# A decoder layer on one core: the start of VectorE's work reordered, a second tile taken without norms, and a last product over four held chunks

## The chip, the cores and the metric

One Trainium2 chip, one of its cores. The metric is the device time of one execution in microseconds (us). The kernel before took 766.85 us (median of 3 runs, 766.26 to 767.05). One more execution was profiled: it took 766.03 us, of which the trace covers 764.2 us from the first to the last instruction.

A core has five engines that run side by side, each through its own queue in order: TensorE (PE, matmuls; PEld is its weight load), VectorE (DVE), ScalarE (ACT), GpSimd (POOL) and SyncE (SP, which here issues the transfers). They wait for each other through semaphores.

## The reference

The layer norms `x` (512 rows of 1024), multiplies it with one wide matrix, mixes tokens in three branches, adds the result to `x`, and then runs a gated MLP. Cut to what matters here:

```python
h = rms_norm(x, g_mix)
proj = h @ w_in
q, k, v, qi, ki, wi, conv_in, qc, gate_pre = split_cols(proj, PROJ_SIZES)
qi, ki = partial_rope(qi, ...), partial_rope(ki, ...)      # the indexer: it picks 128 keys per query
y_att = dsa_attention(q, k, v, qi, ki, wi) @ w_att_out
bg, cg, u = jnp.split(conv_in, 3, axis=-1)                 # 384 channels each: three tiles of 128
y_conv = (bg * causal_dwconv(cg * u, conv_w_short)) @ w_conv_out
y_mem = memory_attention(qc, km, vm) @ w_mem_out
x = x + merged @ w_o
up = causal_dwconv(rms_norm(x, g_ffn) @ w_up, conv_w_ffn)
x = x + (silu(gate) * val) @ w_down
return rms_norm(x, g_final)
```

The norm of a row of `x` is one number per row, so `(x*g) @ w` times that number is the same as `h @ w`.

## The kernel before, in words

Activations lie turned, channels on the 128 partitions and the 512 rows along the free axis. Every operand of a large product is split into a high and a low part (`hi` on ACT by a copy, L160 and L361 and L368; `lo` on DVE by a subtraction, L161, L362, L369), and a product is three matmuls: high by high, low by high, high by low (L150 to L152). A projection of one tile of 128 output channels (`project`, L460) is thus 8 chunks of 3 = 24 matmuls of 512 columns into one PSUM bank. The banks come in three pools: `mm` with 3, `at` with 4, `o` with 1. In the first part one `mm` bank (and `o`) holds the memory's keys and values until ACT reads them at L515 and L516, so two `mm` banks are left for the projections, and a projection waits until the bank it takes has been read.

The order of work. Up to L450 most instructions are in the order in which they are written (`keep`); after that a scheduler sets the order. What is written:

- The rows' norms come out as `rb` (one number per row, on all partitions) and `rx`. The values `v` and the indexer's operands are a product `pn` of unnormed `x` (`xh`, `xl`) that is multiplied by `rx` later.
- `h_split` (L356) makes one of eight chunks of `h`: DVE multiplies (L360), ACT copies the high part (L361), DVE subtracts (L362), each step waiting for the one before.
- The first tile of `cg` (`C_CG`) is taken from unnormed `x` (L409 to L413), and `cg0` is that times `rb` (L430). All other tiles are `project(...)` of `h`: `C_U`, `C_BG`, then the second tiles `C_CG + P`, `C_U + P` and so on (L578 to L596).
- The indexer's rows `rn` are scaled, get the rotary step (L422 to L427), are turned by PE (L433 to L439), and are laid out as `K4` and `Q4`: 16 copies of 32 partitions on ACT (L504) and 19 small transfers on SP. PE then scores them (L525).
- After its product the second tile of `cg` is read from its bank by ACT (`rr`, L585).

At the end `stream_rows` (L814) multiplies `act` with `w_down`: 22 chunks of weights stream through three buffers; for the first 19 chunks PE goes over all 8 output banks per chunk, the last 3 chunks are held, and PE finishes one bank after the other. `after_down` (L903) then adds the bank to `x`, squares and sums on ACT (L910), takes the power on POOL (L918), and writes the normed rows (L919, L920).

Of the kernel before, what the change touches and what calls it, by code (L numbers as in the profile page):

```python
# [93 lines left out]
def layer(ctx, tc, x, mem, g_ffn, g_final, w_in, x_n, m_kv, w_cm, w_att, w_o, w_up, w_down,  # L94
# [314 lines left out]
    pc = bank()  # L409
    for k in range(KD):  # L410
        wh, wl = (x[:, k, :] for x in ready[C_CG])
        for i, (a, b) in enumerate(((wh, xh[k]), (wh, xl[k]), (wl, xh[k]))):
            keep(nc.tensor.matmul(pc, a, b, start=k == 0 and i == 0, stop=k == KD - 1 and i == 2))  # L413
# [19 lines left out]
    for t in range(3):  # L433
        pt = bank("at")
        for b in range(NB):
            if t == 2:
# [3 lines left out]
        if t == 2:  # L440
            keep(nc.scalar.activation(rK, pt[:IDXD], AF.Copy))
        else:
            keep(nc.scalar.activation(rQ[:, t, :], pt[:, :SQ], AF.Copy))
    for b in range(NB):
        v = pn[b][:, :KV].rearrange("p (g d) -> p g d", g=NG)
        nc.scalar.activation(V[:, b, :, 0:HD], v, AF.Copy, scale=rx[:, b:b + 1])
        nc.vector.scalar_tensor_tensor(V[:, b, :, HD:], v, rx[:, b:b + 1], V[:, b, :, 0:HD].bitcast(F32), op0=ALU.mult,
                                       op1=ALU.subtract)
        nc.vector.tensor_scalar(wiN[:, b, :], pn[b][:, NW - NIH:NW], rx[:, b:b + 1], (NIH * IDXD) ** -0.5, op0=ALU.mult,
                                op1=ALU.mult)  # L450
# [527 lines left out]
```

## Time and profile before

| what | value |
|---|---|
| median of 3 runs | 766.85 us |
| profiled execution: own time, span of its trace | 766.03 us, 764.2 us |
| PE busy | 745.3 us (98%), 3443 matmuls |
| DVE busy | 473.2 us (62%) |
| ACT busy | 346.9 us (45%) |
| mean granted TensorE clock | 0.991 of full speed |

PE is busy for nearly the whole span, so the time can only shrink where PE is idle, runs at its lower clock, or has already ended. The profile shows three such places: a stretch between 42 and 78 us, the first microseconds, and the last 8 us behind the last matmul. The views used below are the busy time by stretch, the waits by engine, and the timeline. In a timeline a number behind the start is the duration; engines overlap the end of one instruction with the start of the next, so what an instruction costs in a row of its kind is the distance between two starts. `[2.19 <-ACT rr L585]` is idle time before the row, and who ended it.

### The profile page before, as it was taken

The page shows a single profiled execution, that of the slowest core. Times are in us where ns is not written, and L with a number is a line of the kernel's source. Part 1 is how long each engine was busy: PE and PEld are TensorE (multiplying, and loading weights), DVE is VectorE, ACT ScalarE, POOL GpSimd, SP SyncE. Part 2 cuts the span into 40 slices and gives each one's busy share as a digit, 9 for nine tenths or more (in the row PEclk, how much of TensorE's full clock was granted, in tenths as well). Part 3 has the DMA queues.
Part 4 walks back from the last instruction along what each step waited for, and adds up shares of the span by engine and source line. Part 5 has one row for each costly group of instructions (what it writes and reads, how often), then busy time and mean ns, then how long its engine had stood idle before and what let it go on. Part 6 is the DMA issues. An engine that isn't in the chain of part 4 may idle for free.

```text
span 764.2 us, 9125 instructions
## 1 busy us (share of the span) xinstructions
PE 745.3 (98%) x3443; PEld 620.8 (81%) x3443; DVE 473.2 (62%) x798; ACT 346.9 (45%) x576; POOL 18.0 (2%) x42
## 2 busy tenths in 40 slices
PE   9977999999999999999999999999999999999995
PEld 7955888888888888888889888888888888888884
DVE  5675899999677765367365656565656664222225
ACT  7649465657455653234335343434343433121214
POOL 0000002000000000000010000000000000000001
PEclk9998999999999999999999999999999999999998
DMA  9725233532221223443502223332222232323212
GB/s 344 283 78 163 78 104 117 156 107 72 73 83 65 71 74 107 155 133 108 193 28 84 90 104 90 103 93 100 97 97 98 95 101 70 124 92 100 93 29 110
DMA packets 25965, 83.38 MB, mean 109 GB/s; under 512 B 3297, under 2 KB 4449, under 8 KB 25921
## 3 DMA queue, kind: packets, MB, share of 16 engines
q1 hardware_dynamic: 25776, 82.53, 32.6%
q8 instruction: 27, 0.44, 0.2%
q10 hardware_dynamic: 144, 0.26, 0.1%
q14 instruction: 18, 0.14, 0.1%
HBM read 77.34 MB, written 2.10 MB: 104 GB/s over the span
## 4 chain that ended last, share of the span: by engine, by line
PE 88%; ACT 3%; DVE 2%; issue 1%; POOL 0%; POOLq 0%; ACTq 0%
PE ps_mm L150 18%; PE ps_mm L151 18%; PE ps_mm L152 18%; PE ps_at L150 9%; PE ps_at L152 9%; PE ps_at L151 9%; ACT Q L504 1%; PE ps_at L733 1%; PE ps_o L764 1%; PE ps_at L750 1%; PE ps_o L152 1%; PE ps_o L151 1%; PE ps_o L150 1%; PE ps_at L664 0%; PE ps_o L702 0%
## 5 line engine op out<-in xcount | busy, mean ns | idle before, releaser
L161 DVE TENSOR_TENSOR wlo<-raw,whi 128x1024 fp32r<-128x1024 f32 (+2 forms) x122 | 144.9, 1188 | 193.1 <-ACT whi L160 193.0
L160 ACT ACTIVATE whi<-raw 128x1024 fp32r<-128x1024 f32 (+2 forms) x122 | 125.7, 1031 | 184.6 <-PE ps_o L152 81.9
L150 PE MATMUL ps_mm<-hhi,whi 128*128 128x512 f32 x304 | 120.8, 397 | 3.8 <-ACT rr L585 2.2
L152 PE MATMUL ps_mm<-hhi,wlo 128*128 128x512 f32 x304 | 120.3, 396 | 0.3 <-DVE wlo L369 0.3
L151 PE MATMUL ps_mm<-hlo,whi 128*128 128x512 f32 x304 | 120.3, 396 | 0.2 <-DVE hlo L362 0.2
L151 PE MATMUL ps_at<-h2l,whi 128*128 128x512 f32 (+1 forms) x216 | 78.9, 366 | 0.0
L152 PE MATMUL ps_at<-h2h,wlo 128*128 128x512 f32 (+1 forms) x216 | 78.8, 365 | 0.0
L150 PE MATMUL ps_at<-h2h,whi 128*128 128x512 f32 (+1 forms) x216 | 78.7, 366 | 0.0
L150 PEld LDWEIGHTS ps_mm<-hhi,whi 128*128 128x128 f32 x304 | 57.8, 190 | 16.3 <-ACT rr L585 2.4
L152 PEld LDWEIGHTS ps_mm<-hhi,wlo 128*128 128x128 f32 x304 | 57.8, 190 | 12.4 <-DVE wlo L369 0.7
L151 PEld LDWEIGHTS ps_mm<-hlo,whi 128*128 128x128 f32 x304 | 57.8, 190 | 12.1 <-DVE hlo L362 0.5
L150 PE MATMUL ps_mm<-h2h,whi 128*128 128x512 f32 x160 | 62.2, 389 | 0.0
L151 PE MATMUL ps_mm<-h2l,whi 128*128 128x512 f32 x160 | 62.2, 389 | 0.0
L152 PE MATMUL ps_mm<-h2h,wlo 128*128 128x512 f32 x160 | 62.2, 389 | 0.0
L151 PEld LDWEIGHTS ps_at<-h2l,whi 128*128 128x128 f32 x216 | 40.8, 189 | 6.6
L152 PEld LDWEIGHTS ps_at<-h2h,wlo 128*128 128x128 f32 x216 | 40.8, 189 | 6.5
L150 PEld LDWEIGHTS ps_at<-h2h,whi 128*128 128x128 f32 x216 | 40.6, 189 | 6.5
L151 PEld LDWEIGHTS ps_mm<-h2l,whi 128*128 128x128 f32 x160 | 30.0, 188 | 6.3
L150 PEld LDWEIGHTS ps_mm<-h2h,whi 128*128 128x128 f32 x160 | 30.0, 188 | 6.2
L152 PEld LDWEIGHTS ps_mm<-h2h,wlo 128*128 128x128 f32 x160 | 30.0, 188 | 6.2
L897 ACT ACTIVATE t<-t 128x512 f32<-128x512 f32 x22 | 13.9, 633 | 44.5 <-DVE t L576 44.4
L160 ACT ACTIVATE acth<-t 128x512 fp32r<-128x512 f32 x14 | 8.8, 632 | 40.5 <-DVE t L898 40.5
(288 smaller groups left out, 1325.6 us busy)
## 6 DMA issues: line engine op xcount, KB each, us to landing
raw<-w_up SPq DMA_DIRECT2D x44, 512.0 KB, 3.5
raw<-w_in SPq DMA_DIRECT2D x39, 512.0 KB, 3.3
raw<-w_down SPq DMA_DIRECT2D x22, 512.0 KB, 3.5
raw<-w_o SPq DMA_DIRECT2D x8, 512.0 KB, 3.6
xn<-x_n SPq DMA_DIRECT2D x3, 937.0 KB, 12.2
raw<-w_cm SPq DMA_DIRECT2D x8, 320.0 KB, 3.0
rows<-x SPq DMA_DIRECT2D x4, 512.0 KB, 12.1
x<-x SPq DMA_DIRECT2D x4, 512.0 KB, 5.4
```

Of the source, the lines that this page charges most:

```text
L150: nc.tensor.matmul(o, sh, mh, start=first, stop=False)
L151: nc.tensor.matmul(o, sh, ml, start=False, stop=False)
L152: nc.tensor.matmul(o, sl, mh, start=False, stop=last)
L160: nc.scalar.activation(hi, src, AF.Copy)
L161: nc.vector.tensor_sub(lo, src, hi.bitcast(F32))
L504: nc.scalar.activation(Q4[32 * i:32 * i + 32, 4 * t + j, :], r[src], AF.Copy)
L733: nc.tensor.matmul(pb[:, :N], QS[:, hd, b * P:(b + 1) * P], KS[i][:, g, :N], start=(i == 0), stop=(i == 1))
L750: nc.tensor.transpose(pt[:, kb * P:(kb + 1) * P], lt[:, kb * P:(kb + 1) * P], ident)
L764: nc.tensor.matmul(po[:, q0:], V[:, kb, g, :], PT[i][:, c], start=(kb == 0 and i == 0), stop=(kb == NB - 1 and i == 1))
L897: nc.scalar.activation(tt[0], tt[0], AF.Silu)
```

## The change

`h` is built in a pipeline: `h_split` is taken apart into `h_rows` (multiply, copy) and `h_low` (subtract), and a piece's subtraction is written behind a later piece's multiplication. `ahead` (split of a weight tile) is likewise taken apart into `split_hi` (ACT) and `split_lo` (DVE). The first tile of `C_U` is now also taken from unnormed `x` (`bare`), as that of `C_CG` was; `cg0` becomes both products times `rb` twice, one DVE multiplication more. The rotary step, the turning and the layout of the indexer's operands stand earlier or in another order, and two second tiles of weights (`C_CG + P`, `C_U + P`) are loaded in the written part. In the last product 4 chunks are held instead of 3, in buffers of their own (those of `h2`), and the last bank is finished in two halves of 256 columns, the second half in a bank of its own.

```diff
     early(C_BG)
+    early(C_CG + P)
+    early(C_U + P)
...
-    def h_split(*ks):
-
-        for k in ks:
-            xt = xn[k // 2][:, k % 2, :S]
-            keep(nc.vector.scalar_tensor_tensor(xt, xt, xn[k // 2][:, k % 2, S + NW:], rb, op0=ALU.mult, op1=ALU.mult))
-            keep(nc.scalar.activation(h[0][:, k], xt, AF.Copy))
-            keep(nc.vector.tensor_sub(h[1][:, k], xt, h[0][:, k].bitcast(F32)))
+    def h_rows(k):
+
+        xt = xn[k // 2][:, k % 2, :S]
+        keep(nc.vector.scalar_tensor_tensor(xt, xt, xn[k // 2][:, k % 2, S + NW:], rb, op0=ALU.mult, op1=ALU.mult))
+        keep(nc.scalar.activation(h[0][:, k], xt, AF.Copy))
+
+    def h_low(k):
+        xt = xn[k // 2][:, k % 2, :S]
+        keep(nc.vector.tensor_sub(h[1][:, k], xt, h[0][:, k].bitcast(F32)))
...
-    h_split(0)
+    h_rows(0)
+    split_hi(C_CG)
     cols_split(3, [0, 1])
     rows_products(6, 7)
-    h_split(1)
-    ahead(C_CG)
-    h_split(2, 3, 4)
+    h_rows(1)
+    h_low(0)
+    split_lo(C_CG)
+    h_rows(2)
+    h_low(1)
+    h_rows(3)
+    h_low(2)
+    split_hi(C_U)
+
+    def bare(c0, ks):
+        pb = bare_banks.setdefault(c0, None) or bank()
+        bare_banks[c0] = pb
+        for k in ks:
+            wh, wl = (x[:, k, :] for x in ready[c0])
+            for i, (a, b) in enumerate(((wh, xh[k]), (wh, xl[k]), (wl, xh[k]))):
+                keep(nc.tensor.matmul(pb, a, b, start=k == 0 and i == 0, stop=k == KD - 1 and i == 2))
+        return pb
...
-    ahead(C_U)
-    h_split(5)
+    vs = [pn[b][:, :KV].rearrange("p (g d) -> p g d", g=NG) for b in range(NB)]
+    for b in range(NB):
+        keep(nc.scalar.activation(V[:, b, :, 0:HD], vs[b], AF.Copy, scale=rx[:, b:b + 1]))
+    split_lo(C_U)
...
+    h_rows(4)
     keep(nc.vector.tensor_mul(cg0, pc, rb))
-    h_split(6, 7)
-    ahead(C_BG)
+    h_low(3)
+    split_hi(C_BG)
+    h_low(4)
+    bare(C_U, range(5))
...
+    pu0 = bare(C_U, range(5, KD))
...
+    split_lo(C_BG)
+    h_rows(5)
+    h_rows(6)
+    h_low(5)
+    h_rows(7)
+    h_low(6)
+    keep(nc.vector.tensor_mul(cg0, pu0, cg0))
+    h_low(7)
+    split_hi(C_CG + P)
+    split_lo(C_CG + P)
+    keep(nc.vector.tensor_mul(cg0, cg0, rb))
...
+    qls = [halves(rQ[:, t, :], ip, SQ)[1] for t in range(2)]
+    split_hi(C_U + P)
+    split_lo(C_U + P)
     for t in range(2):
...
-                nc.scalar.activation(Q4[32 * i:32 * i + 32, 4 * t + j, :], r[src], AF.Copy)
+                keep(nc.scalar.activation(Q4[32 * i:32 * i + 32, 4 * t + j, :], r[src], AF.Copy))
...
+                fin = fine and (b, hf) == (NB - 1, 1)
+                n = 256 if fin else 512
                 for i, wt in enumerate(last):
-                    step(b, kc - tail + i, wt, hf)
-                done(b, hf * 512, hf * 512 + 512, acc[b][hf])
+                    step(b, kc - tail + i, wt, hf, 0, n)
+                done(b, hf * 512, hf * 512 + n, acc[b][hf][:, :n])
+                if fin:
+                    rest = bank("at")[:, :n]
+                    for i, wt in enumerate(last):
+                        step(b, kc - tail + i, wt, hf, n, 512, rest, kc - tail)
+                    nc.vector.tensor_add(x1[:, b, D - n:], acc[b][hf][:, n:], x1[:, b, D - n:])
+                    done(b, D - n, D, rest)
...
-        nc.vector.tensor_mul(xs, xs, gl[:, c0:c1])
+
+        xg = fp.tile([P, 512], F32, tag="t0", name="xg", bufs=2)
+        tc.keep_in_program_order(nc.vector.tensor_mul(xg, x1[:, b, 512:], gl[:, 512:]))
+        nc.vector.tensor_add(st[:, 0:1], st[:, 0:1], s1)
...
-    stream_rows(w_down, act, NF, 3, after_down, wp)
+    tails = [h2p.tile([P, 4, KD, P], F32R, tag=n, name="t" + n) for n in ("h2h", "h2l")]
...
+    stream_rows(w_down, act, NF, 4, after_down, hold, fine=True)
```

How this moves the instructions. On PE, behind the unnormed product of `C_CG` (matmuls from `xg` with `whi`, `wlo`), this stood before: the normed product of `C_U` (from `hhi`, `hlo`) begins at once, and the turning of the indexer's rows `rn` stands after its second matmul.

```order
L413 MATMUL ps_mm<-xg_268,wlo 128x512
L150 MATMUL ps_mm<-hhi,whi 128x512
L151 MATMUL ps_mm<-hlo,whi 128x512
L439 MATMUL ps_at<-ident,rn 128x128 x6
L437 MATMUL ps_at<-ident,rn 32x128 x4
L152 MATMUL ps_mm<-hhi,wlo 128x512
L150 MATMUL ps_mm<-hhi,whi 128x512
```

At the same place now; the first normed product is that of `C_BG`.

```order
L430 MATMUL ps_mm<-xg,wlo 128x512
L469 MATMUL ps_at<-ident,rn 32x128 x4
L471 MATMUL ps_at<-ident,rn 128x128 x6
L430 MATMUL ps_mm<-xg,whi 128x512 x2
L430 MATMUL ps_mm<-xg,wlo 128x512
L430 MATMUL ps_mm<-xg_272,whi 128x512
L430 MATMUL ps_mm<-xg_273,whi 128x512
L430 MATMUL ps_mm<-xg_272,wlo 128x512
L430 MATMUL ps_mm<-xg_272,whi 128x512
L430 MATMUL ps_mm<-xg_273,whi 128x512
L430 MATMUL ps_mm<-xg_272,wlo 128x512
L150 MATMUL ps_mm<-hhi,whi 128x512
```

The turning stands 15 matmuls into a second unnormed product, and no normed product stands ahead of it any more.

On ACT this stood between the indexer's layout (`hvh`, `Q`, `K`) and the reading of the second `cg` tile's bank (`rr`), before:

```order
L504 ACTIVATE Q_538<-rQ 32x384 x11
L493 ACTIVATE K_539<-rK 32x512
L504 ACTIVATE Q_538<-rQ 32x384 x4
L160 ACTIVATE hvh<-rQ 128x384
L504 ACTIVATE Q_538<-rQ 32x384
L287 ACTIVATE rows,ss<-rows 128x1024
L160 ACTIVATE whi<-raw 128x1024
L287 ACTIVATE rows,ss<-rows 128x1024
L590 ACTIVATE rs<-rb,par 128x512
L160 ACTIVATE whi<-raw 128x1024
L585 ACTIVATE rr<-ps_mm 128x512
```

And now:

```order
L160 ACTIVATE hvh<-rQ 128x384
L372 ACTIVATE whi<-raw 128x1024
L160 ACTIVATE whi<-raw 128x1024
L544 ACTIVATE Q_573<-rQ 32x384 x15
L160 ACTIVATE whi<-raw 128x1024
L544 ACTIVATE Q_573<-rQ 32x384
L289 ACTIVATE rows,ss<-rows 128x1024 x2
L160 ACTIVATE ocvh<-rs 128x512
L625 ACTIVATE rr<-ps_mm 128x512
```

Both `hvh` and the first splits stand ahead of the 16 copies; `rr` still stands behind all of them.

On DVE the stretch from the rotary step (`rt`, `rn`) to the indexer's low parts (`kl`, `hvl`) has 32 instructions now. Its middle, the pieces of `h` (`xn` multiply, `hlo` subtract), stood like this before, each `hlo` right behind its `xn`:

```order
L360 SCALAR_TENSOR_TENSOR xn_145<-xn_145,rb 128x512
L362 TENSOR_TENSOR hlo<-xn_145,hhi 128x512
L430 TENSOR_TENSOR rb<-ps_mm,rb 128x512
L360 SCALAR_TENSOR_TENSOR xn_146<-xn_146,rb 128x512
L362 TENSOR_TENSOR hlo<-xn_146,hhi 128x512
L360 SCALAR_TENSOR_TENSOR xn_146<-xn_146,rb 128x512
L362 TENSOR_TENSOR hlo<-xn_146,hhi 128x512
```

And now:

```order
L377 TENSOR_TENSOR wlo<-raw,whi 128x1024
L361 SCALAR_TENSOR_TENSOR xn_145<-xn_145,rb 128x512
L361 SCALAR_TENSOR_TENSOR xn_146<-xn_146,rb 128x512
L366 TENSOR_TENSOR hlo<-xn_145,hhi 128x512
L361 SCALAR_TENSOR_TENSOR xn_146<-xn_146,rb 128x512
L366 TENSOR_TENSOR hlo<-xn_146,hhi 128x512
L483 TENSOR_TENSOR rb<-ps_mm,rb 128x512
L366 TENSOR_TENSOR hlo<-xn_146,hhi 128x512
```

A piece's subtraction now has another DVE instruction between it and its own multiplication.

## Rows read from the trace of the kernel before

**Rows 1.** Busy time by stretch: length, then busy (instructions) of each engine, clock, DMA.
```profile
40.00:60.00 20.00, 15.46 (x63) 11.46 (x62) 16.38 (x33) 11.37 (x22) 0.00 (x0) 0.91 0.29 88
60.00:80.00 20.00, 14.96 (x57) 11.58 (x56) 9.24 (x15) 16.06 (x32) 0.90 (x2) 0.83 0.49 146
80.00:180.00 100.00, 100.00 (x470) 83.58 (x469) 97.43 (x213) 62.48 (x119) 6.21 (x4) 1.00 0.35 107
```
**Rows 2.** Waits of PE: who waited for whom, us in total, times, longest.
```profile
PE ps_at L439 <- DVE rn L427: 2.4, 1, 2.4
PE ps_mm L150 <- ACT rr L585: 2.2, 1, 2.2
```
**Rows 3.** Timeline of PE behind its wait: start, duration, instruction [idle before, releaser].
```profile
73.28 0.79 PE L150 MATMUL ps_mm<-hhi,whi 128*128 128x512 f32 x1 [2.19 <-ACT rr L585]
...
77.71 0.39 PE L151 MATMUL ps_mm<-hlo,whi 128*128 128x512 f32 x1
77.94 0.39 PE L152 MATMUL ps_mm<-hhi,wlo 128*128 128x512 f32 x1
```
**Rows 4.** Timeline of ACT ahead of that wait.
```profile
57.85 0.51 ACT L160 ACTIVATE hvh<-rQ 128x384 fp32r<-128x384 f32 x1
58.27 5.87 ACT L504 ACTIVATE Q<-rQ 32x384 fp32r<-32x384 f32 x11
...
68.05 1.06 ACT L287 ACTIVATE rows<-rows 128x1024 f32<-128x1024 f32 x1
...
69.11 1.04 ACT L160 ACTIVATE whi<-raw 128x1024 fp32r<-128x1024 f32 x1
...
72.66 0.57 ACT L585 ACTIVATE rr<-ps_mm 128x512 f32<-128x512 f32 x1
```
**Rows 5.** Waits of all engines between 28 and 76 us.
```profile
DVE hlo L362 <- ACT hhi L361: 5.6, 8, 0.7
```
**Rows 6.** Timeline of DVE from the rotary step on.
```profile
43.61 0.31 DVE L422 TENSOR_TENSOR rt<-rn,ropeN 128x144 f32<-128x144 f32 x1
...
45.20 0.21 DVE L449 TENSOR_SCALAR wiN<-ps_at,rx 128x8 f32<-128x8 f32 x1
45.34 0.34 DVE L447 SCALAR_TENSOR_TENSOR v<-ps_at,rx,v 128x128 fp32r<-128x128 f32 x1
...
46.42 0.30 DVE L427 TENSOR_TENSOR rn<-rn,rt 128x144 f32<-128x144 f32 x1
46.64 1.21 DVE L369 TENSOR_TENSOR wlo<-raw,whi 128x1024 fp32r<-128x1024 f32 x1
47.77 0.74 DVE L360 SCALAR_TENSOR_TENSOR xn<-xn,rb 128x512 f32<-128x512 f32 x1
49.21 0.69 DVE L362 TENSOR_TENSOR hlo<-xn,hhi 128x512 fp32r<-128x512 f32 x1 [0.69 <-ACT hhi L361]
49.82 0.68 DVE L430 TENSOR_TENSOR rb<-ps_mm,rb 128x512 f32<-128x512 f32 x1
```
**Rows 7.** Timeline of the end, behind the last matmul.
```profile
756.60 0.69 DVE L909 TENSOR_TENSOR x<-ps_o,x 128x512 f32<-128x512 f32 x1
...
757.32 0.63 ACT L910 ACTIVATE y<-x 128x512 f32<-128x512 f32 x1 [0.25 <-DVE x L909]
...
758.08 0.16 DVE L914 TENSOR_TENSOR st<-st,sq 128x1 f32<-128x1 f32 x1 [0.73 <-ACT y L910]
...
758.32 0.92 POOL L918 TENSOR_TENSOR st<-st,mhalf 128x1 f32<-128x1 f32 x1 [2.61 <-DVE st L914]
...
759.27 0.75 DVE L919 SCALAR_TENSOR_TENSOR y<-x,st,gl 128x512 f32<-128x512 f32 x1 [0.44 <-POOL st L918]
```
**Rows 8.** Timeline of POOL: the first block's power.
```profile
750.89 0.54 POOL L918 TENSOR_TENSOR st<-st,mhalf 128x1 f32<-128x1 f32 x1 [352.59 <-DVE st L912]
```
**Rows 9.** Timeline of PE: twelve matmuls of 256 columns in a row.
```profile
151.28 1.60 PE L664 MATMUL ps_at<-km,QC 128*128 128x256 f32 x12
```
**Rows 10.** Transfers by line: KB each, median us from issue to landing.
```profile
raw<-w_down SPq DMA_DIRECT2D x22, 512.0 KB, 3.5
```

More of the change, by code (lines that the diff above doesn't have):

```diff
@@ L354, in rows_products, with split_hi @@
                 rows_product(k, part)
-    def h_split(*ks):
-        for k in ks:
-            xt = xn[k // 2][:, k % 2, :S]
-            keep(nc.vector.scalar_tensor_tensor(xt, xt, xn[k // 2][:, k % 2, S + NW:], rb, op0=ALU.mult, op1=ALU.mult))
-            keep(nc.scalar.activation(h[0][:, k], xt, AF.Copy))
-            keep(nc.vector.tensor_sub(h[1][:, k], xt, h[0][:, k].bitcast(F32)))
-    def ahead(c0):
+    def h_rows(k):
[5 more added lines that the diff above has]
+        keep(nc.vector.tensor_sub(h[1][:, k], xt, h[0][:, k].bitcast(F32)))
+    def split_hi(c0):
         raw = ready[c0]
@@ L368, in ahead, with split_lo @@
         keep(nc.scalar.activation(hi, raw, AF.Copy))
+        ready[c0] = hi, lo, raw
+    def split_lo(c0):
+        hi, lo, raw = ready[c0]
         keep(nc.vector.tensor_sub(lo, raw, hi.bitcast(F32)))
@@ L401, in layer @@
     rows_products(4, 5)
-    h_split(0)
+    h_rows(0)
+    split_hi(C_CG)
     cols_split(3, [0, 1])
     rows_products(6, 7)
-    h_split(1)
-    ahead(C_CG)
-    h_split(2, 3, 4)
[L409 to L413, printed above, removed]
+    h_rows(1)
[14 more added lines that the diff above has]
+        return pb
+    bare_banks = {}
+    pc = bare(C_CG, range(KD))
     rn = ea.tile([P, NB, NIH + 1, IDXD], F32, name="rn")
@@ L427, in layer @@
     keep(nc.vector.tensor_add(a2, a2, rt[:, 1]))
-    ahead(C_U)
-    h_split(5)
-    keep(nc.vector.tensor_mul(cg0, pc, rb))
-    h_split(6, 7)
-    ahead(C_BG)
-    for t in range(3):
-        pt = bank("at")
+    vs = [pn[b][:, :KV].rearrange("p (g d) -> p g d", g=NG) for b in range(NB)]
+    for b in range(NB):
+        keep(nc.scalar.activation(V[:, b, :, 0:HD], vs[b], AF.Copy, scale=rx[:, b:b + 1]))
+    split_lo(C_U)
+    for b in range(NB):
+        keep(nc.vector.scalar_tensor_tensor(V[:, b, :, HD:], vs[b], rx[:, b:b + 1], V[:, b, :, 0:HD].bitcast(F32), op0=ALU.mult,
+                                            op1=ALU.subtract))
+        keep(nc.vector.tensor_scalar(wiN[:, b, :], pn[b][:, NW - NIH:NW], rx[:, b:b + 1], (NIH * IDXD) ** -0.5, op0=ALU.mult,
+                                     op1=ALU.mult))
@@ L435, in layer @@
+    h_rows(4)
+    keep(nc.vector.tensor_mul(cg0, pc, rb))
+    h_low(3)
+    split_hi(C_BG)
+    h_low(4)
+    bare(C_U, range(5))
+    pts = {}
+    for t in (2, 0, 1):
+        pt = pts[t] = bank("at")
         for b in range(NB):
             if t == 2:
-                nc.tensor.transpose(pt[:IDXD, b * P:(b + 1) * P], rn[:, b, NIH, :], ident)
+                keep(nc.tensor.transpose(pt[:IDXD, b * P:(b + 1) * P], rn[:, b, NIH, :], ident))
             elif b:
-                nc.tensor.transpose(pt[:, (b - 1) * P:b * P], rn[:, b, 4 * t:4 * t + 4, :].rearrange("p n d -> p (n d)"), ident)
@@ L440, in layer @@
[L440 to L450, printed above, removed]
+                keep(nc.tensor.transpose(pt[:, (b - 1) * P:b * P], rn[:, b, 4 * t:4 * t + 4, :].rearrange("p n d -> p (n d)"),
+                                         ident))
@@ L451, in twice @@
+    pu0 = bare(C_U, range(5, KD))
+    keep(nc.scalar.activation(rK, pts[2][:IDXD], AF.Copy))
+    for t in range(2):
+        keep(nc.scalar.activation(rQ[:, t, :], pts[t][:, :SQ], AF.Copy))
+    split_lo(C_BG)
[9 more added lines that the diff above has]
+    keep(nc.vector.tensor_mul(cg0, cg0, rb))
     def twice(K, r, j, hd, lo):
@@ L586, in layer @@
         pump(3)
-        pu = project(C_U + c * P)
-        nc.vector.tensor_mul(cg, pu, cg)
+        if c:
+            pu = project(C_U + c * P)
+            nc.vector.tensor_mul(cg, pu, cg)
         t = rp.tile([P, S], F32, tag="rs", name="rs", bufs=2)
@@ L811, in layer, with stream_rows, step @@
         nc.sync.dma_start(x1[:, b, :], x[b * P:(b + 1) * P, :])
-    def stream_rows(w, act, kc, tail, done, sp):
+    def stream_rows(w, act, kc, tail, done, hold, fine=False):
         tags = ["at"] * 4 + ["mm"] * 3 + ["o"]
         acc = [[bank(tags[2 * b + i]) for i in range(2)] for b in range(NB)]
-        def step(b, k, wt, hf):
+        def step(b, k, wt, hf, c0=0, c1=512, po=None, k0=0):
             bs = slice(b * P, (b + 1) * P)
-            mh, ml = (x.rearrange("p k c -> p (k c)")[:, hf * 512:hf * 512 + 512] for x in wt)
-            mm3(acc[b][hf], act(0, k)[:, bs], act(1, k)[:, bs], mh, ml, k == 0, k == kc - 1)
+            mh, ml = (x.rearrange("p k c -> p (k c)")[:, hf * 512 + c0:hf * 512 + c1] for x in wt)
+            po = acc[b][hf][:, c0:c1] if po is None else po
+            mm3(po, act(0, k)[:, bs], act(1, k)[:, bs], mh, ml, k == k0, k == kc - 1)
         for k in range(kc - tail):
@@ L827, in stream_rows @@
                     step(b, k, wt, hf)
-        last = [wrows(w, k, sp) for k in range(kc - tail, kc)]
+        last = [hold(k - kc + tail, w[k * P:(k + 1) * P, :]) for k in range(kc - tail, kc)]
         for b in range(NB):
             for hf in range(2):
+                fin = fine and (b, hf) == (NB - 1, 1)
+                n = 256 if fin else 512
                 for i, wt in enumerate(last):
-                    step(b, kc - tail + i, wt, hf)
-                done(b, hf * 512, hf * 512 + 512, acc[b][hf])
+                    step(b, kc - tail + i, wt, hf, 0, n)
[6 more added lines that the diff above has]
+                    done(b, D - n, D, rest)
     h2p = hs.enter_context(pool("h2p"))
-    h2 = (h2p.tile([P, KD, S], F32R, name="h2h"), h2p.tile([P, KD, S], F32R, name="h2l"))
+    h2 = (h2p.tile([P, KD, S], F32R, tag="h2h", name="h2h"), h2p.tile([P, KD, S], F32R, tag="h2l", name="h2l"))
     ns = ExitStack()
@@ L905, in after_down @@
         if c0 == 0:
-            down[b] = (fp.tile([P, 2], F32, tag="st", name="st", bufs=4), fp.tile([P, 2], F32, tag="sq", name="sq", bufs=4),
+            down[b] = (fp.tile([P, 2], F32, tag="st", name="st", bufs=4), fp.tile([P, 3], F32, tag="sq", name="sq", bufs=4),
                        fp.tile([P, D], F32, tag="y", name="y", bufs=4))
         st, sq, y = down[b]
+        s1 = sq[:, (0, 512, 768).index(c0):][:, :1]
         nc.vector.tensor_add(xs, acc, xs)
-        nc.scalar.activation(y[:, c0:c1], xs, AF.Square, scale=D ** -0.5, accum_out=sq[:, 0:1] if c0 == 0 else sq[:, 1:2])
+        nc.scalar.activation(y[:, c0:c1], xs, AF.Square, scale=D ** -0.5, accum_out=s1)
         if c0 == 0:
-            nc.vector.tensor_scalar_add(st[:, 0:1], sq[:, 0:1], EPS)
-        else:
-            nc.vector.tensor_add(st[:, 0:1], st[:, 0:1], sq[:, 1:2])
+            nc.vector.tensor_scalar_add(st[:, 0:1], s1, EPS)
+        elif c1 < D:
+            nc.vector.tensor_add(st[:, 0:1], st[:, 0:1], s1)
         if c1 < D:
             return
-        nc.vector.tensor_mul(xs, xs, gl[:, c0:c1])
+        xg = fp.tile([P, 512], F32, tag="t0", name="xg", bufs=2)
+        tc.keep_in_program_order(nc.vector.tensor_mul(xg, x1[:, b, 512:], gl[:, 512:]))
+        nc.vector.tensor_add(st[:, 0:1], st[:, 0:1], s1)
         nc.gpsimd.tensor_tensor(out=st[:, 1:2], in0=st[:, 0:1], in1=mhalf, op=ALU.pow)
-        nc.vector.scalar_tensor_tensor(y[:, :c0], x1[:, b, :c0], st[:, 1:2], gl[:, :c0], op0=ALU.mult, op1=ALU.mult)
-        nc.scalar.activation(y[:, c0:], xs, AF.Copy, scale=st[:, 1:2])
+        nc.vector.scalar_tensor_tensor(y[:, :512], x1[:, b, :512], st[:, 1:2], gl[:, :512], op0=ALU.mult, op1=ALU.mult)
+        nc.scalar.activation(y[:, 512:], xg, AF.Copy, scale=st[:, 1:2])
         if b < NB - 1:
@@ L923, in after_down, with hold @@
         else:
-            nc.scalar.dma_start(out[b * P:(b + 1) * P, c0:], y[:, c0:])
-            nc.sync.dma_start(out[b * P:(b + 1) * P, :c0], y[:, :c0])
-    stream_rows(w_down, act, NF, 3, after_down, wp)
+            nc.scalar.dma_start(out[b * P:(b + 1) * P, 512:], y[:, 512:])
+            nc.sync.dma_start(out[b * P:(b + 1) * P, :512], y[:, :512])
+    tails = [h2p.tile([P, 4, KD, P], F32R, tag=n, name="t" + n) for n in ("h2h", "h2l")]
+    def hold(i, src):
+        raw = load(src.rearrange("p (k c) -> p k c", c=P))
+        with tc.high_priority(offset=400):
+            split(tails[0][:, i], tails[1][:, i], raw)
+        return tails[0][:, i], tails[1][:, i]
+    stream_rows(w_down, act, NF, 4, after_down, hold, fine=True)
     hs.close()
```

7 lines of the change are left out of this document (3 added, 4 removed).

## The prediction

> **What bounds the kernel now.** I read the busy time by stretch first. From 80 to 180 us PE has no idle time and its full clock, as it has in nearly the whole span; only 40 to 60 and 60 to 80 us show PE at 15.46 and 14.96 of 20 us, with granted clocks of 0.91 and 0.83 [rows 1]. So the front of the kernel is the one place inside the span where time can be had, and a step there is worth only what it does to the wait that ends last. That is in the waits of PE: 2.4 us for the rotary step and, later, 2.2 us for ACT's reading of a bank (`rr`) [rows 2]. The later one decides. At 73.28 us PE begins the second tile of `C_U`; behind it there is no wait of PE until the end [rows 2, 3]. Whatever PE loses before 73.28 us is given back in that wait, so I do not add up the waits before it. By then PE has done four projections (`C_CG`, `C_U`, `C_BG`, `C_CG + P`), the turning and five scores of the indexer. The timeline of ACT says why `rr` is late: 16 copies of 32 partitions at 0.53 us each (eleven take 5.87 us), two sums of squares and four splits stand ahead of it [rows 4]. The last place is the end: from the last bank's addition at 756.60 us to the last normed row at 759.27 us four engines work in turn, with PE done [rows 7].
>
> **The change: the front.** I follow the new order to the same event, ACT's `rr`, and count what PE has done by then.
>
> *To the rotary step.* Before, its first row starts at 43.61 us [rows 6]. In the new order one subtraction, one multiplication and one subtraction of `h` (`hlo`, `xn`, `hlo`) go behind it: 0.61 + 0.67 + 0.61 = 1.9 us, by the distance of two starts (49.21 to 49.82, and 0.74 less the overlap of 0.07) [rows 6]. Four of the eight waits of 0.70 us of a subtraction for its high part lie here and go, since another DVE instruction stands between: 2.8 us, and 0.3 us of overlap that each wait had cost [rows 5]. Against that, ACT's split of a weight tile (0.95 us) now stands ahead of the split of the last weights of `pn`, which DVE waits for; a subtraction (0.61 us) that stood ahead comes behind; and the rotary step waits some 0.9 us for ACT's two scalings, queued behind the split of `C_U`. 43.61 - 1.9 - 3.1 + 0.95 + 0.6 + 0.9 = 41.1; following ACT instead (third high part, split 0.95, two scalings) gives 40.7. I take 40.8 us.
>
> *To the indexer's low part.* From there to `hvl` stand 32 DVE instructions, none of which should wait: 6 of the rotary step at 0.22, 3 splits at 1.13, 4 pairs for `v` and `wi` at 0.26 + 0.14, 4 `xn` at 0.67, 5 `hlo` at 0.61, 3 products with `rb` at 0.60 (one of them the multiplication that the change adds), and `bgT`, `kl`, `hvl` at 0.1 + 0.6 + 0.55 [rows 6]: 1.3 + 3.4 + 1.6 + 2.7 + 3.05 + 1.8 + 1.25 = 15.1 us, so 55.9 us.
>
> *To `rr`.* ACT's second `hvh` waits for that, and behind it ACT never waits: 0.42 for `hvh`, 2 splits at 0.95, 15 copies at 0.53, a split, a copy, two sums of squares at 1.06, a high part at 0.54, `rr` at 0.57 [rows 4]: 0.42 + 1.9 + 8.0 + 0.95 + 0.53 + 2.1 + 0.54 + 0.57 = 15.0 us. With 0.2 us for changes of engine on the way PE goes on at **71.2 us**, 2.1 us earlier than 73.28.
>
> *What PE has done by then.* The two unnormed products need no `h`, so the 2.4 us wait for the rotary step goes and the turning is done inside the second. Five projections are done (`C_U + P` too) and again five scores. One projection is 24 matmuls at 0.227 us (77.71 to 77.94) [rows 3], 5.4 us. PE needs until about 68.2 us for it: 73.28 less the 4.5 + 5.0 us in which it was idle, less (1 - 0.91) x 20 = 1.8 us lost to the first fall of the clock [rows 1], plus 5.4 us for the fifth and some 0.8 us of a new wait for the split of `C_U`. So it waits 3 to 4 us for `rr`. This cover hides PE's own delays ahead of it, the new wait included; without it each would count in full. The front gives 2.1 + 5.4 = **7.5 us**.
>
> *The clock.* Before, PE's ten matmuls from 73.28 to 77.71 us stand 0.44 us apart [rows 3], at 1.2 GHz, after a stretch of waits; the next ones at 2.4 GHz. That cost 4.43 - 10 x 0.23 = 2.1 us. In the new order PE waits as long in one piece, so I expect the same fall and the same ten slow matmuls: no difference. Bounds: the clock does not fall (2.1 us more gain), or its whole low stretch, (1 - 0.83) x 20 x 2 = 6.8 us [rows 1], lies on work: 3.4 us lost, 1.3 us less gain.
>
> *At nothing.* The two written loads are the ones that the scheduler put at the same two places of SP's queue; SP has nothing else to issue there. The indexer's 19 small transfers go out while PE works on `C_CG + P` and `C_U + P`; before they were what the scores waited for, now `rr` is later. If `rr` were early they would cost up to 1 us.
>
> **The change: the end.** The last half has 256 columns. From the addition to the normed row before: 2.67 us [rows 7]. Now the addition is 0.69 - 0.26 = 0.43 us (half of the 0.52 us between 1024 and 512 columns of a DVE subtraction [rows 6]), then the product with the gain at 0.09 + 0.61 (it stands ahead of the sum now, and hides the shorter square), the sum at 0.16, the power and two handoffs of 0.05. The power took 0.92 us there, beside a DVE product of two SBUF tiles, and 0.54 us beside an addition from PSUM [rows 7, 8]; now DVE is idle beside it. That gives 1.9 to 2.3 us, 0.4 to 0.8 less; I take 0.6. The last bank's twelve matmuls become 24 of 256 columns at 0.12 us (the next matmul starts 1.44 us after twelve began [rows 9]): 0.16 us more. Four held chunks cost PE nothing while they land in time. The end gives **0.4 us**.
>
> **A rule against it.** Adjacent starts on DVE lie closer than the durations: 46.64 to 47.77 for 1.21 us [rows 6]. The Trainium skill ("VectorE: DVE Perf Modes", section "The DRAIN you can't avoid") says that the next operation cannot issue until the pipe is empty; it adds that one that is not held starts earlier. By its first sentence the 32 instructions would take 0.08 us more each, 2.6 us, and the sum would be 5.3 us. The rows show the overlap, so the sum stays.
>
> **Sum.** 7.5 + 0 + 0.4 = 7.9 us off the profiled execution's 766.03 us gives 758.1 us; the median of the runs lies 0.8 us higher, so I predict **759.0 us**.
>
> **Rivals.**
> 1. *The forecast*, 759.0 us, its own range 757.6 to 760.8 us: chance 0.62.
> 2. *The clock stays up, or `rr` comes earlier.* 2.1 us more: 756.9 us. For it: the first stretch of waits cost only half as long a low clock as the second (0.91 against 0.83) [rows 1]. Against it: one wait of 3 to 4 us is longer than any that went before a fall here, 2.4 us [rows 2]. Chance 0.13.
> 3. *The pipeline on DVE does not hold.* If the five subtractions ahead of `hvl` still wait 0.70 us each [rows 5], or the 32 instructions lose their overlap of 0.08 us each, `rr` is 2.6 to 3.5 us later: 761.6 to 762.5 us. For it: ACT's high parts stand behind splits of 0.95 us, which can be late. Against it: a multiplication or a split of DVE lies in each gap. Chance 0.19.
> 4. *Slower: the fourth held chunk is late.* At the last product, PE stands still before the first held bank if loads and splits do not come in time; a load takes 3.5 us [rows 10] and its two splits about 0.95 + 1.13. Two late chunks cost up to 11.2 us: 759.0 + 11.2 = 770.2 us; it decides from 7.9 us on. Against it: a streamed chunk keeps PE busy for 24 matmuls, 5.4 us, about as long as one chunk needs, and the held ones have buffers of their own. Chance 0.03. DVE is no such rival although it is 97.43 of 100 us busy from 80 to 180 us [rows 1]: it gets one instruction more.
> 5. *Nothing changes*, the saved wait comes back in full at `rr`: the projection done meanwhile would have to wait as well. 766.5 us, chance 0.03.
>
> A measurement of this kernel can tell about 0.2% (1.5 us) from no change. The cases give faster 0.94, within it 0.03, slower 0.03. The range takes in rival 2, and rival 3 but for its far end: 756.8 to 762.2 us.
>
> **What would show it.** In the profile after: no wait of PE for the rotary step; one wait for `rr` of 3 to 4 us that ends near 71.2 us with the matmuls of `C_BG + P` behind it; slow matmuls for some 4 us; no wait between 80 us and the end; about 2.1 us from the last half's addition to the last row. I am wrong if PE's long wait ends after 73 us, if the subtractions still wait for their high parts, or if PE waits at the held chunks.

## The result and the profile after

The changed kernel takes 757.99 us (median of 4 runs, 757.26 to 758.25), the kernel before took 766.56 us beside it (4 runs). The ratio is 0.9886, 95% interval 0.9869 to 0.9903: 8.6 us less, where 7.9 were forecast. The profiled execution took 758.25 us, with a span of 756.5 us and a mean granted clock of 0.997; PE is busy for 742.5 us of it.

The busy time by stretch (columns as in [rows 1]):

```profile
40.00:60.00 20.00, 19.70 (x92) 15.85 (x91) 18.96 (x39) 13.11 (x24) 0.00 (x0) 1.00 0.38 121
60.00:80.00 20.00, 15.62 (x66) 12.72 (x65) 10.56 (x18) 17.25 (x36) 0.90 (x2) 0.91 0.44 140
80.00:180.00 100.00, 100.00 (x472) 83.51 (x472) 99.00 (x220) 63.98 (x128) 5.86 (x4) 1.00 0.35 106
```

Against [rows 1] the first stretch is full now, 19.70 of 20 us at full clock. In the second PE is busy for 15.62 us instead of 14.96, yet does 66 matmuls instead of 57: the clock is 0.91 and not 0.83. All waits of PE (us in total, times, longest):

```profile
PE ps_mm L150 <- ACT rr L625: 4.4, 1, 4.4
PE ps_at L246 <- POOL ident masks.py:199: 1.5, 1, 1.5
PE ps_o L319 <- ACT mT L309: 0.3, 1, 0.3
PE ps_mm L430 <- DVE wlo L377: 0.3, 1, 0.3
PE ps_at L350 <- ACT xg L341: 0.3, 1, 0.3
```

The wait for the rotary step [rows 2] is gone, and PE does not wait at the held chunks. One long wait is left in the stretch from 42 to 78 us, and it is the one for ACT's reading of the bank (`rr`). PE's timeline around it, which answers to [rows 3]:

```profile
67.21 0.51 PE L565 MATMUL ps_at<-K,Q 128*128 128x256 f32 x3
72.11 0.80 PE L150 MATMUL ps_mm<-hhi,whi 128*128 128x512 f32 x1 [4.38 <-ACT rr L625]
...
75.26 0.45 PE L151 MATMUL ps_mm<-hlo,whi 128*128 128x512 f32 x1
75.55 0.40 PE L152 MATMUL ps_mm<-hhi,wlo 128*128 128x512 f32 x1
```

PE goes on at 72.11 us with the matmuls of `C_BG + P`; eight of them take 72.11 to 75.55 us, 0.43 us each at 1.2 GHz (the granted clock is 0.52 of full speed from 72.1 to 75.5 us), and then the clock is at 2.4 GHz again (1.00 from 75.6 to 80 us). ACT ahead of that point, which answers to [rows 4]:

```profile
55.73 0.72 ACT L631 ACTIVATE rs<-rb,par 128x512 f32<-128x512 f32 x1 [1.07 <-issue]
56.82 0.53 ACT L160 ACTIVATE hvh<-rQ 128x384 fp32r<-128x384 f32 x1 [0.37 <-DVE hvl L161]
...
59.15 8.06 ACT L544 ACTIVATE Q<-rQ 32x384 fp32r<-32x384 f32 x15
...
68.86 1.06 ACT L289 ACTIVATE rows<-rows 128x1024 f32<-128x1024 f32 x1
...
71.48 0.58 ACT L625 ACTIVATE rr<-ps_mm 128x512 f32<-128x512 f32 x1
```

From `hvh` on ACT does not wait, and `rr` (71.48 to 72.06 us) is what PE goes on behind. DVE from the rotary step to the indexer's low part, which answers to [rows 6]:

```profile
41.56 0.31 DVE L443 TENSOR_TENSOR rt<-rn,ropeN 128x144 f32<-128x144 f32 x1 [0.97 <-ACT rn L439]
...
45.71 0.74 DVE L361 SCALAR_TENSOR_TENSOR xn<-xn,rb 128x512 f32<-128x512 f32 x1
46.37 0.68 DVE L459 TENSOR_TENSOR rb<-ps_mm,rb 128x512 f32<-128x512 f32 x1
46.97 1.28 DVE L366 TENSOR_TENSOR hlo<-xn,hhi 128x512 fp32r<-128x512 f32 x2
...
56.25 0.54 DVE L161 TENSOR_TENSOR hvl<-rQ,hvh 128x384 fp32r<-128x384 f32 x1
56.72 0.73 DVE L615 SCALAR_TENSOR_TENSOR rs<-rb,par,rs 128x511 f32<-128x511 f32 x1
```

None of these 32 instructions waits for a high part; the whole stretch takes 56.72 - 41.56 = 15.16 us. The end, which answers to [rows 7]:

```profile
749.59 0.42 DVE L961 TENSOR_TENSOR x<-ps_at,x 128x256 f32<-128x256 f32 x1 [0.28 <-PE ps_at L152]
...
750.05 0.69 DVE L971 TENSOR_TENSOR xg<-x,gl 128x512 f32<-128x512 f32 x1
750.66 0.15 DVE L972 TENSOR_TENSOR st<-st,sq 128x1 f32<-128x1 f32 x1
750.89 0.54 POOL L973 TENSOR_TENSOR st<-st,mhalf 128x1 f32<-128x1 f32 x1 [4.63 <-DVE st L972]
...
751.47 0.75 DVE L974 SCALAR_TENSOR_TENSOR y<-x,st,gl 128x512 f32<-128x512 f32 x1 [0.66 <-POOL st L973]
```

From the last addition to the last normed row it is 1.88 us, 0.79 less than before.

### The profile page after: what moved, and what is told of

Read it like the earlier page. It is cut to its first block, busy times and chain, and to the rows that moved or that the text cites. A ratio compares the mean times of both kernels' runs of the same rounds, so it can differ in the third digit from the quotient of the medians.

```text
span 756.5 us, 9156 instructions
## 1 busy us (share of the span) xinstructions
PE 742.5 (98%) x3455; PEld 620.0 (82%) x3455; DVE 475.1 (63%) x802; ACT 346.9 (46%) x578; POOL 16.5 (2%) x42
## 4 chain that ended last, share of the span: by engine, by line
PE 89%; DVE 3%; ACT 3%; DMA 3%; issue 1%; SPq 0%; POOLq 0%; POOL 0%; ACTq 0%
PE ps_mm L150 18%; PE ps_mm L151 18%; PE ps_mm L152 18%; PE ps_at L152 9%; PE ps_at L150 9%; PE ps_at L151 9%; DMA xn<-x_n 2%; DMA mkv<-m_kv 1%; ACT Q L544 1%; PE ps_o L805 1%; PE ps_at L774 1%; PE ps_at L791 1%; PE ps_o L152 1%; PE ps_o L151 1%; PE ps_o L150 1%
## 5 line engine op out<-in xcount | busy, mean ns | idle before, releaser
L161 DVE TENSOR_TENSOR wlo<-raw,whi 128x1024 fp32r<-128x1024 f32 (+2 forms) x116 | 137.4, 1186 | 172.4 <-ACT whi L160 172.1
L160 ACT ACTIVATE whi<-raw 128x1024 fp32r<-128x1024 f32 (+2 forms) x116 | 119.5, 1031 | 161.5 <-PE ps_mm L151 68.4
L150 PE MATMUL ps_mm<-hhi,whi 128*128 128x512 f32 x296 | 116.9, 396 | 4.4 <-ACT rr L625 4.4
L151 PE MATMUL ps_mm<-hlo,whi 128*128 128x512 f32 x296 | 116.6, 395 | 0.0
L152 PE MATMUL ps_mm<-hhi,wlo 128*128 128x512 f32 x296 | 116.0, 393 | 0.0
L150 PEld LDWEIGHTS ps_mm<-hhi,whi 128*128 128x128 f32 x296 | 56.0, 189 | 15.7 <-ACT rr L625 4.6
L152 PEld LDWEIGHTS ps_mm<-hhi,wlo 128*128 128x128 f32 x296 | 55.9, 189 | 11.4
L151 PEld LDWEIGHTS ps_mm<-hlo,whi 128*128 128x128 f32 x296 | 56.1, 189 | 10.8
```

What stands on the lines that cost most here:

```text
L150: nc.tensor.matmul(o, sh, mh, start=first, stop=False)
L151: nc.tensor.matmul(o, sh, ml, start=False, stop=False)
L152: nc.tensor.matmul(o, sl, mh, start=False, stop=last)
L160: nc.scalar.activation(hi, src, AF.Copy)
L161: nc.vector.tensor_sub(lo, src, hi.bitcast(F32))
```

## The experiments

Medians in us; each ratio is to the kernel before on the same chip (766.46 to 766.70 us there), with its 95% interval. Differences between kernels below are differences of these medians.

| kernel | median | ratio |
|---|---|---|
| 1 only the end | 765.88 | 0.9990 (0.9981 to 0.9999) |
| 2 only the front | 759.28 | 0.9901 (0.9888 to 0.9915) |
| 3 whole, banks read by VectorE | 751.68 | 0.9803 (0.9790 to 0.9817) |
| 4 whole, no pipeline | 762.81 | 0.9950 (0.9936 to 0.9963) |
| 5 whole, first `u` tile normed | 762.85 | 0.9957 (0.9943 to 0.9971) |
| 6 as 5, banks read by VectorE | 755.87 | 0.9863 (0.9849 to 0.9876) |
| 7 as 4, banks read by VectorE | 755.05 | 0.9851 (0.9838 to 0.9865) |
| 8 before, banks read by VectorE | 760.69 | 0.9927 (0.9914 to 0.9941) |

**1 and 2. The two halves of the change apart.** In the first, only this and the functions `hold`, `stream_rows` and `after_down` of the diff above; in the second, all but them.

```diff
-    stream_rows(w_down, act, NF, 3, after_down, wp)
+    stream_rows(w_down, act, NF, 4, after_down, hold, fine=True)
```

> Only the end of the change, on the kernel before: four held chunks and the last bank in two halves. Theory: the chain from the last addition to the last normed row takes 1.9 us instead of 2.67, and the 24 short matmuls cost 0.16 us more: 0.4 to 0.6 us less than before, about 766.0 us, with the front as before (the wait for the second cg tile's bank ends near 73 us). Rival: holding a fourth chunk in its own buffers moves loads or splits and changes more than that, by over 1 us in either direction; then a wait of PE shows near the held chunks.

> Only the front of the change, with the end as before. Theory: nearly all of the gain is here: 7.5 to 8.2 us less than before, about 758.6 us, 0.4 to 0.6 us above the whole change. Rival: the front gives no more than 6 us, and the rest of the 8.6 us that was measured comes from the end; then it takes 760.5 us or more.

Measured: 0.8 us less for the end, 7.4 us less for the front, together 8.2 of the 8.6 us. Neither rival shows: nearly all of the gain is in the front. Both sizes miss by a little: the end was to give 0.4 to 0.6 us, and its interval (0.1 to 1.5 us) is too wide to tell 0.4 from 0.8; the front was to give 7.5 to 8.2 us and lies 1.3 us above the whole change instead of 0.4 to 0.6. The trace of the end alone has the 1.88 us behind the last addition, and no wait of PE at the held chunks.

**3. The bank read by another engine.** ACT's queue is taken out of the way, nothing else.

```diff
             cg = rp.tile([P, S], F32, tag="rr", name="rr", bufs=2)
-            nc.scalar.activation(cg, pc, AF.Copy)
+            nc.vector.tensor_copy(cg, pc)
```

> The whole change, but the bank of the second and third cg tile is read by VectorE instead of ScalarE. Theory (what holds PE is only that this reading stands behind 16 copies on ScalarE): PE's wait of 4.4 us and the slow matmuls behind it (1.6 us) go, VectorE pays 0.6 us once more in each tile: 4 to 6 us less than the whole change, 752 to 754 us, and the granted clock stays at 1.00 from 60 to 80 us. Rival 1 (VectorE, 99% busy from 80 to 180 us, is the bound just behind): what is won at 72 us is given back by 180 us, at most 1.5 us less, 756.5 us or more, with waits of PE for VectorE between 80 and 180 us. Rival 2 (the scores or their small transfers are late next): 2 to 3 us less, with a wait of PE for transfers.

Measured: 751.68 us, 6.3 less than the whole change, a little over the theory's 4 to 6. In its windows PE is full and at its upper clock from 60 us on, and DVE is as busy from 80 to 180 us as after the whole change (99.00):

```profile
60.00:80.00 20.00, 20.00 (x94) 16.64 (x93) 12.79 (x21) 18.36 (x37) 0.90 (x2) 1.00 0.44 137
80.00:180.00 100.00, 100.00 (x476) 83.48 (x475) 98.95 (x220) 68.55 (x135) 5.94 (x4) 1.00 0.36 112
```

DVE reads the bank as soon as PE has filled it, ten us ahead of ACT's 71.48; the second row is the third tile's bank:

```profile
61.19 0.69 DVE L625 COPY rr<-ps_mm 128x512 f32<-128x512 f32 x1 [0.24 <-PE ps_mm L152]
...
79.95 0.68 DVE L625 COPY rr<-ps_mm 128x512 f32<-128x512 f32 x1
```

So the price of that queue is the wait and the slow matmuls behind it: 4.38 + (3.44 - 8 x 0.23) = 6.0 us. The two profiled executions differ by 758.25 - 751.68 = 6.57 us; 0.52 us of that is an earlier start (DVE's product of the third weights, `wnl`, stands at 26.44 us here and at 26.96 after the change). Rival 1 falls: PE has no wait in the 100 us in which DVE is 99% busy. But both copies stand ahead of that stretch, where DVE has room (12.79 of 20 us busy), so this does not test a DVE that is full. Rival 2 falls: no score waits for a transfer. This version beats both kernels, by 15.0 us and 6.3 us.

**4. No pipeline.** Each `h_low` stands right behind its `h_rows`; the diff shows two of the eight.

```diff
     h_rows(2)
-    h_low(1)
+    h_low(2)
     h_rows(3)
-    h_low(2)
+    h_low(3)
...
```

> The whole change without the pipeline: each subtraction of h stands right behind its own multiplication again. Theory: the waits of 0.70 us for the high parts come back, those ahead of the indexer's low part count in full for ScalarE's reading of the bank: PE's long wait ends 2.6 to 4 us later, 760.6 to 762.0 us, while the waits ahead of the rotary step are covered by the unnormed products or add under 1 us. Rival 1: all nine waits add up, 6 us, 764 us. Rival 2: the order of ScalarE alone sets that end, and the pipeline is worth under 0.5 us.

Measured: 762.81 us, 0.8 us above the theory's range and below rival 1. The waits are back, and PE goes on 3.7 us later; first the line of DVE's waits, then two rows of PE's timeline:

```profile
DVE hlo L366 <- ACT hhi L362: 6.1, 8, 1.2
```

```profile
45.06 0.50 PE L431 MATMUL ps_mm<-xg,wlo 128*128 128x512 f32 x1 [1.81 <-DVE wlo L377]
...
75.82 0.80 PE L150 MATMUL ps_mm<-hhi,whi 128*128 128x512 f32 x1 [5.45 <-ACT rr L625]
```

I had called the waits ahead of the rotary step covered. They are covered on PE, but they stand on DVE's own way to `hvl`: this execution reached the product of the third weights (`wnl`) at 26.15 us against 26.96 after the change, so at an equal start PE goes on 3.71 + 0.81 = 4.5 us later. 1.6 us of it is there at the rotary step already (42.34 against 41.56 us, and the 0.81), 2.95 us come between it and `hvl` (17.64 us instead of 14.69). Ten matmuls are slow behind the wait instead of eight.

```profile
42.34 0.31 DVE L444 TENSOR_TENSOR rt<-rn,ropeN 128x144 f32<-128x144 f32 x1 [0.18 <-ACT rn L440]
...
59.98 0.54 DVE L161 TENSOR_TENSOR hvl<-rQ,hvh 128x384 fp32r<-128x384 f32 x1
```

**5 and 6. The first tile of `u` from the normed `h`**, with ACT and with DVE reading the later banks.

```diff
-    bare(C_U, range(5))
...
-    pu0 = bare(C_U, range(5, KD))
...
-    keep(nc.vector.tensor_mul(cg0, pu0, cg0))
...
-    keep(nc.vector.tensor_mul(cg0, cg0, rb))
...
-        if c:
-            pu = project(C_U + c * P)
-            nc.vector.tensor_mul(cg, pu, cg)
+        pu = project(C_U + c * P)
+        nc.vector.tensor_mul(cg, pu, cg)
```

> The whole change, but the first tile of u is taken from the normed h again (h is still built in the pipeline). Theory: PE has to wait for pieces of h, the product with cg0 comes later, the bank of bg is read later, and only four instead of five projections are done before the second cg tile's bank is read: 4 to 6 us more than the whole change, 762 to 764 us. Rival: the 4.4 us wait in front of the bank hides PE's waits for h: under 1 us more, 758 to 759 us.

> The same (first u tile from normed h), with the banks of the later cg tiles read by VectorE. Theory: with the queue of ScalarE no longer in the way, PE's waits for h and for the indexer count themselves: some 2 us for h and 2 to 3 us at the scores, 4 to 6 us more than with the unnormed tile, 755.5 to 758 us. Rival: the unnormed tile is worth something only through the bank, so it costs under 1 us here, 752.5 us or less.

Measured: 762.85 us, 4.9 us more than the whole change, and 755.87 us, 4.2 more than experiment 3: both in the theory's ranges. In experiment 5 PE has done four projections when it stops for ACT. It stops at a score, whose bank ACT reads (`rl`) right ahead of `rr` in its queue, and the matmuls of the fifth projection start as soon as `rr` has ended; first PE's rows, then ACT's queue:

```profile
71.14 1.12 PE L561 MATMUL ps_at<-K,Q 128*128 128x256 f32 x3 [6.05 <-ACT rl L566]
72.17 0.80 PE L150 MATMUL ps_mm<-hhi,whi 128*128 128x512 f32 x1
```

```profile
58.48 8.57 ACT L540 ACTIVATE Q<-rQ 32x384 fp32r<-32x384 f32 x16
...
69.17 0.71 ACT L626 ACTIVATE rs<-rb,par 128x512 f32<-128x512 f32 x1
...
71.52 0.60 ACT L621 ACTIVATE rr<-ps_mm 128x512 f32<-128x512 f32 x1
```

So PE goes on at the same time as after the whole change (72.11 us), one projection of 5.4 us behind. The row of `rs` tells why the unnormed tile allows a fifth projection. The bank of `C_BG` comes free only when the convolution's first tap (`rs`) is ready for DVE's product with it. After the change `cg0` is ready early, `rs` runs at 55.73 us, ahead of the copies of `Q`, and that bank is free some 0.7 us after 59.65 us:

```profile
59.65 0.68 DVE L635 TENSOR_TENSOR rs<-ps_mm,rs 128x512 f32<-128x512 f32 x1
```

With the normed tile `rs` stands behind the copies, at 69.17 us, as it did before, and DVE's product starts at 72.90 us. This is read from the traces; no run moved `rs` alone. In experiment 6 my split was off: the scores wait 1.5 us, a piece of `h`, a split and the banks 1.3 us in four waits; the rest of the 4.2 us I did not place.

**7. No pipeline, banks read by DVE** (the edits of 3 and 4).

> No pipeline (each subtraction right behind its multiplication), with the banks of the later cg tiles read by VectorE. Theory: the waits of 0.7 us no longer move the bank's reading; what is left is PE's own wait of 1.8 us for the split of the first u tile and about 1.4 us of short waits for pieces of h, and up to 1.8 us of slow matmuls: 754 to 756.5 us, against 751.7 us with the pipeline. Rival: they were felt through ScalarE's queue alone, 752.5 us or less.

Measured: 755.05 us, 3.4 more than experiment 3, as the theory said. PE's one long wait in the front is the one for the split of `C_U`, and the clock is 0.91 from 40 to 60 us:

```profile
PE ps_mm L431 <- DVE wlo L377: 1.9, 1, 1.9
```

The pipeline is thus worth 4.8 us where ACT's queue ends last, and 3.4 us where it does not.

**8. The kernel before with that one line changed.**

```diff
-        nc.scalar.activation(cg, pc, AF.Copy)
+        nc.vector.tensor_copy(cg, pc)
```

> The kernel before with one line changed: VectorE reads the banks of the later cg tiles. Theory: the wait of 2.2 us and the slow stretch behind it go, but PE's earlier waits (4.5 us and 5.0 us), which the last wait had hidden in part, stay: 3 to 5 us less than before, 761.5 to 763.7 us. Rival 1: this one line does what the reordering does, 754 us or less. Rival 2: the waits for the indexer's small transfers take its place, 766 us.

Measured: 760.69 us, 5.8 less than before and 0.8 better than the theory's range. Three losses go at once, not two: the wait of 2.2 us, the slow matmuls' 2.1 us, and the scores' two waits for `Q` of 1.4 us in all, since the scheduler put the scores in among the matmuls of the next projection. From 60 to 80 us PE has its full clock:

```profile
60.00:80.00 20.00, 18.36 (x83) 14.72 (x82) 11.56 (x18) 17.99 (x35) 0.90 (x2) 1.00 0.52 153
```

Rival 1 falls: the other waits stay (2.4 us for the rotary step, 1.7 for a split, 1.4 for `K`). So with DVE reading, the whole change is still worth 9.0 us.

**9 and 10. The end.** On experiment 3, the product with the gain behind the sum, or the last bank in one piece; one execution each.

```diff
-        tc.keep_in_program_order(nc.vector.tensor_mul(xg, x1[:, b, 512:], gl[:, 512:]))
-        nc.vector.tensor_add(st[:, 0:1], st[:, 0:1], s1)
+        tc.keep_in_program_order(nc.vector.tensor_add(st[:, 0:1], st[:, 0:1], s1))
+        tc.keep_in_program_order(nc.vector.tensor_mul(xg, x1[:, b, 512:], gl[:, 512:]))
```

```diff
-    stream_rows(w_down, act, NF, 4, after_down, hold, fine=True)
+    stream_rows(w_down, act, NF, 4, after_down, hold)
```

> The whole change with the banks read by VectorE, and in the last row block the product with the gain written behind the sum, so that VectorE multiplies two tiles of SBUF while GpSimd takes the power. Theory (the power is slow beside such a product): the power of the last row block takes 0.9 to 1.0 us instead of 0.55, and from the last addition to the last normed row it is 2.2 to 2.3 us instead of 1.88. Rival (the two durations of the power had another cause): it stays at 0.55 us, and the stretch at 1.85 to 1.95 us.

> The whole change with the banks read by VectorE, and the last bank finished in one piece of 512 columns (four chunks held as before). Theory: from the last addition to the last normed row it is 0.25 us (addition) plus 0.2 us (longer square) more, 2.3 us, and the matmuls of the last bank take 0.16 us less. Rival: the sum, not the square, sets the power's start, and it is 2.1 us or less.

Experiment 9's last block:

```profile
742.83 0.42 DVE L961 TENSOR_TENSOR x<-ps_at,x 128x256 f32<-128x256 f32 x1 [0.21 <-PE ps_at L152]
...
743.90 0.69 DVE L972 TENSOR_TENSOR xg<-x,gl 128x512 f32<-128x512 f32 x1
744.07 0.93 POOL L973 TENSOR_TENSOR st<-st,mhalf 128x1 f32<-128x1 f32 x1 [4.19 <-DVE st L971]
...
745.03 0.75 DVE L974 SCALAR_TENSOR_TENSOR y<-x,st,gl 128x512 f32<-128x512 f32 x1 [0.44 <-POOL st L973]
```

The same power takes 0.93 us beside `xg` and 0.54 us without it, and the stretch is 2.20 us, 0.32 more than the 1.88 us of experiment 3. Experiment 10's:

```profile
742.68 0.69 DVE L961 TENSOR_TENSOR x<-ps_o,x 128x512 f32<-128x512 f32 x1 [0.85 <-PE ps_o L152]
...
744.98 0.75 DVE L974 SCALAR_TENSOR_TENSOR y<-x,st,gl 128x512 f32<-128x512 f32 x1 [0.66 <-POOL st L973]
```

2.30 us in one piece. Both theories hold: of the 0.79 us, 0.42 come from the half piece (2.30 to 1.88). The other 0.37 (2.67 to 2.30) go with the order of the product and the sum, which is worth 0.32 us by itself in experiment 9. Both executions took 751.8 us in all, where such sizes don't show.

## Why the prediction was right

**The event that counts.** Right: the time follows the end of PE's wait for `rr`, as it did before, and experiment 3 shows that nothing else in the front holds PE by more than 0.3 us.

**To the rotary step, to the low part, to `rr`.** Right nearly to the digit, apart from the start. The third split's low part (`wnl`) stands at 26.96 us here and stood at 26.07 us before, with the same wait of 1.61 us: the execution is 0.9 us late by then.

```profile
26.07 1.04 DVE L340 TENSOR_TENSOR wnl<-xn,wnh 128x848 fp32r<-128x848 f32 x1 [1.61 <-ACT wnh L337]
```

```profile
26.96 1.04 DVE L342 TENSOR_TENSOR wnl<-xn,wnh 128x848 fp32r<-128x848 f32 x1 [1.61 <-ACT wnh L339]
```

With 0.9 us added, 40.8 becomes 41.7 us (41.56 measured), 55.9 becomes 56.8 (`hvl` ends at 56.79), 15.0 us of ACT are 15.24, and 71.2 becomes 72.1 us (72.11). In the profiled executions of all kernels here that row lies between 26.07 and 27.00 us: 26.07 to 26.18 with the old front, 26.15 to 27.00 with the new one. All kernels with the new front have the same program up to that row, so executions alone differ by up to 0.85 us there. Whether the change adds a shift of its own stays open.

**What PE has done by then.** Five projections and five scores, as forecast; the reason was only half told, since it also takes the early `rs` (experiment 5). The prediction gave no row for when the fifth projection's bank comes free (rival 5 names the danger, and no more), so that it came free in time was in part luck. PE's idle time is 4.38 us, not 3 to 4. PE was ready at 72.11 - 4.38 = 67.7 us; 68.2 and the later start of 0.9 would have been 69.1, 1.4 us more; 0.5 of that is the wait for the split of `C_U`, 0.30 instead of 0.8 us; the rest was not traced. The cover made it cost nothing, as the prediction said it would.

**The clock: off by a size.** The same fall came, but eight matmuls were slow and not ten: 1.6 us lost instead of 2.1. Rival 2's full clock did not come.

**The end.** 0.79 less the 0.16 us of the short matmuls, 0.63 us instead of 0.4; the power was the uncertain part, and it took its shorter time (0.54 us).

**The sum.** For the profiled executions: 7.5 - 0.9 (start) + 0.5 (clock) + 0.63 = 7.73 us, measured 766.03 - 758.25 = 7.78. That this is so near the forecast 7.9 us is in part luck: the late start takes away what the clock and the end give beyond the forecast. What missed is the last step, the median as 0.8 us above the profiled execution: here the execution lies 0.26 us above its median. That is the 1.0 us between 759.0 and 757.99. That the late start puts it there is not shown: the profiled execution of experiment 2 starts as late (27.00 us) and lies 0.32 us below its median.

**The rivals.** The pipeline holds (rival 3): the line of `hlo` waiting for `hhi` [rows 5] is gone, and experiment 4 prices what rival 3 feared at 4.8 us, more than its 2.6 to 3.5, since it took in only the subtractions between the rotary step and `hvl` (2.95 us in experiment 4) and left out those ahead of the rotary step (1.6 us). The fourth held chunk costs nothing (rival 4, experiment 1). The sentence in the Trainium skill's "VectorE: DVE Perf Modes" ("The DRAIN you can't avoid") by which the next operation waits until the pipe is empty would, read alone, have made the 32 instructions some 17.7 us, an estimate (15.16 + 32 x 0.08). The trace's 15.16 us do not agree with that reading: the instructions overlap, as they did before the change.

## What to carry to other kernels

When an engine's last wait is for a small step in another engine's queue, read what stands ahead of that step in the queue: here one line that gave the step to a third engine was worth 6 us on either kernel, as much as most of a large reordering. The third engine could take it because its queue was not late at that point, though it is 99% busy soon after. Whether the step set ahead of the copies in ACT's own queue would have done as well was not run. Follow a chain on the engine that carries it: a wait that is covered on PE still counts in full on DVE if DVE's own chain sets the end. And add the slow matmuls behind a wait of PE to the wait: here 1.6 us to 4.4.

## What was not expected of the hardware

GpSimd's power of 128 numbers takes 0.54 us alone and 0.93 us beside a VectorE product of two SBUF tiles (experiment 9, in which only two VectorE instructions changed places). The granted clock fell after PE's waits of 4.4 us (the change) and 5.4 us (experiment 4), with eight and ten slow matmuls, and after the 1.9 us of experiment 7 (0.91 from 40 to 60 us), but not after the wait of 1.5 us at the scores in experiment 6 (1.00 from 60 to 80 us).
